# A decoder trunk on one core: the first loads cut and reordered, and another order of recurrent units and gates

## The chip, the cores and the metric

The kernel runs on one core of one Trainium2 chip. The metric is the device time in microseconds (us), the median of several runs. Lower is better.

## What is computed

One inference step of a two-layer decoder trunk on 512 prompt rows and 8 x 8 sample rows of width 1024, all in float32. Cut to what bears on this change, the first layer's first half:

```python
def trunk(x, c, ...):                                  # cut to the start
    sh1, sc1, g1, sh2, sc2, g2 = split(silu(c) @ ada_w[l] + ada_b[l], 6)
    h = rms_norm(x, norm_g[l, 0]) * (1 + sc1) + sh1
    xr, yg = split(h @ w_in, 2)                        # 8 + 8 blocks of 128 columns
    xr, new_buf = causal_dwconv(xr, conv_buf, conv_w, conv_b)        # width 4
    g = sigmoid(einsum('btnc,ncd->btnd', xr by blocks, gate_w) + gate_b)   # r and i
    log_a = 8 * r * log_sigmoid(lam)
    a, u = exp(log_a), sqrt(-expm1(2 * log_a)) * (i * xr)
    o = scan(h -> a * h + u)
    x = x + g1 * ((o * gelu(yg)) @ w_out)
    ...                                                # FFN, K/V, layer 1, final norm
```

## The kernel before

**Layout.** The activations are kept turned, channels on the 128 partitions, in two halves `h` = 0 and 1 of 288 columns (256 prompt rows and 32 sample rows). Prompt row tiles 0, 1 and the samples (tile 4) go to half 0, and tiles 2, 3 to half 1. Turning is done by TensorE (`x_turn`), the sum of squares for the norm by `x_half(h)`: on ScalarE for tiles 0 and 2, on VectorE for tiles 1 and 3.

**Products.** Each float32 weight block is split in two float32r tiles, `hi` (a CAST on ScalarE) and `lo` (raw minus hi, a subtraction on VectorE); `convert` does both for one unit, and the tiles are called `wh`. The activations are split the same way. A product takes three matmuls for each of 8 blocks of 128 rows: hi by xh, hi by xl, lo by xh, each 128x288 (in the profile `mm<-h,wh`). `x01` is a unit pair for columns 0 and 1 of `w_in` (its first unit, blocks 0 to 3, stands at the head of the stream of units; it is tile raw2), `quad` holds rows 0 to 255 of columns 3 to 6 (raw3), whose partial products `quad_parts(h)` puts away in `sl` tiles. The unit loads are 384 or 512 KB each.

**Conditioning.** `ada_first(c, m)` makes scale and shift for two blocks of channels c, c+1 from the raw `ada_w` weights: 64 matmuls of 128x32 by 128 into an `ada` tile, then a transpose. Its weights come by `ada_first_load`, eight loads of 256 KB for a pair: p0 (wh1 to wh4), p1 (wh9 to wh12), p2 (reg6 to reg9), p3. `modulated(h, ...)` then makes h01 (half 0) and h11 (half 1). `wh12b` below is the second load of wh12, the last of p1.

**Recurrent stage.** For each block c of channels: `x` (h by w_in, then the convolution, `evac_xr`), `g` (`gates`: ScalarE CAST ta, VectorE subtraction tb, six 128x300 matmuls `mm<-ta,wh` and `mm<-tb,wh`, then two Tanh, and a Tanh and an Exp that are scaled by the tiles sp2 and nsp4), and `y` (`evac_yg`). sp2 and nsp4 come from `decay_rates`: an Exp of 128x8 on ScalarE, a RECIPROCAL on VectorE, and 24 instructions of 128x8 on GpSimd, the last two of which write sp and nsp.

**Order.** All instructions are recorded in program order, and a list scheduler (`Rec.order`, an `Op` each with `prio`, cost, predecessors) writes each engine's fixed order of issue: at each step it takes the instruction that can start soonest by the planner's costs, weighed with its priority, and looks 24 ahead. The word list `LOADS` sets the order of the first loads on SyncE's queue and of the first conversions (p: ada weights, u: the next unit, x2 and x3: those row tiles). `RNN` sets the order in which x, g and y of each block are recorded. `early(n)` moves an instruction's priority by n places. While TensorE would idle by the plan at the start, fills (128x128 matmuls `mm<-ident`, which nobody reads) are put in. SyncE's queue feeds the 16 DMA engines; the loads are spread over eight DMA rings in turn.

Of the kernel before, what the change touches and what calls it, by code (L numbers as in the profile page):

```python
# [16 lines left out]
ALU = mybir.AluOpType  # L17
AX = mybir.AxisListType

P = 128  # L20
D = 1024
KC = D // P
# [29 lines left out]
SPW = 60  # L52
WIN = 600

LOADS = "p0 u x2 x3 u p1 p201 p223 u u p3"
QUAD = (3, 4, 5, 6)
QK = 2
YT = lambda td, ta, sl: td
RNN = "x0 x1 x2 x3 x4 x5 g0 g1 g2 y2 y0 y1 g3 g4 x6 y3 x7 g5 y5 g6 y6 g7 y4 y7"
ATT = "q0A q2A a0A q1A q0B a2A q1B q3A a0B q2B q4A a1A a1B a4A a3A q3B a2B q5A q4B a3B q6A a5A q5B q7A a6A a4B s0A a5B s1A s2A s3A q6B q7B a7A s0B s1B a6B fA a7B o0A s2B s3B o1A o2A fB"  # L60
LOOK = {"PE": 24, "DVE": 24, "ACT": 24, "POOL": 24, "SP": 24}
NRAW = 4
FILL = 250
DKC = 4
XB = 100
NFILL = 60
AE = 100
A0 = 0.0
# [31 lines left out]
def _is_psum(ap):  # L100
    return str(ap.space).endswith("PSUM")


class Op:
    __slots__ = ("i", "prio", "eng", "emit", "cost", "func", "preds", "succ", "npred", "ready", "allocs", "start", "end", "done", "lat", "tiles", "port", "mode", "idle")


class Ref:
# [39 lines left out]
class Recorder:  # L148
# [57 lines left out]
    def add(self, eng, emit, cost, outs, ins, func=None, lat=0, port=False, mode=0):  # L206
        if self.batch is not None:
            self.mode = mode
            self.batch.append((eng, emit, cost, outs, ins))
            return  # L210
        op = Op()
        op.i = len(self.ops)
        op.prio = op.i + self.bias
        op.eng, op.emit, op.cost, op.func, op.lat = eng, emit, cost, func, lat
        op.port, op.mode, op.idle = port, mode, bool(self.fills) and self.fills[-1][2]
        op.preds, op.succ, op.allocs, op.tiles = set(), [], [], set()
        for ap in self.hold:

            op.preds.update(e[0] for e in self.hist[ap.tensor.name] if e[1])
        for ap, wr in [(x, False) for x in ins] + [(x, True) for x in outs]:  # L220
            if str(ap.space).endswith("DRAM"):
                continue
            for n, p0, p1, lo, hi in self.regions(ap):
                if _is_psum(ap):
                    p0, p1, lo, hi = 0, P, 0, 2048
                op.tiles.add(n)
                h = self.hist.setdefault(n, [])
                if n in self.kind_of and n not in op.allocs:
                    op.allocs.append(n)
                keep = []  # L230
                for e in h:
                    q, ewr, a0, a1, b0, b1 = e
                    if (wr or ewr) and q is not op and a0 < p1 and p0 < a1 and b0 < hi and lo < b1:
                        op.preds.add(q)
                        if wr and p0 <= a0 and a1 <= p1 and lo <= b0 and b1 <= hi:
                            continue
                    keep.append(e)
                keep.append((op, wr, p0, p1, lo, hi))
                self.hist[n] = keep
        self.ops.append(op)  # L240
        return op


    def schedule(self):
# [21 lines left out]
        port, holder, mode = 0.0, "", 0  # L266
# [40 lines left out]
        done = set()  # L307
        fills = deque(self.fills)
        while n_left:
# [67 lines left out]
            _, s, op, sw = best  # L377
# [4 lines left out]
            for n in op.allocs:  # L382
                if n in got:
                    continue
                k = self.kind_of[n]
                c = [u for u in slots[k] if u <= s] or slots[k]
# [3 lines left out]
            cost = op.cost  # L390
            if op.port == 1:
                port, holder = s + cost, e
            elif op.port == 2 and s + 60 < port:
                cost += port - s
            if e == "PE":
                mode = op.mode
# [5 lines left out]
            if op.lat:  # L402

                free[e] = s + op.cost
                if e == "POOL":
                    op.end = s + op.cost + (3000 if op.i < self.strict else 5000)
                else:
                    b = max(s + op.cost + 650, dma_free[0])
                    dma_free[0] = b + op.lat
                    op.end = b + op.lat + (2900 if op.i >= self.strict else 2000)  # L410
            else:
                op.end = free[e] = s + cost
            for n in op.tiles:
# [122 lines left out]
def trunk_kernel(ctx, tc, a):  # L536
    nc = tc.nc
    rec = Recorder(a["shadow"])
    V, S, G, T, Q = (Engine(rec, n, o) for n, o in (("DVE", nc.vector), ("ACT", nc.scalar), ("POOL", nc.gpsimd), ("PE", nc.tensor), ("SP", nc.sync)))
# [19 lines left out]
    raws = Slots(rec, cp, "raw", D, NRAW)  # L559
    whs = Slots(rec, cp, "wh", D, 2 * NHI, F32R)  # L560
# [31 lines left out]
    @contextmanager  # L592
    def early(n):

        rec.bias -= n
        yield
        rec.bias += n
# [14 lines left out]
    ab, ng = a["ada_b"].rearrange("l (r p) -> (l r) p", p=P), a["norm_g"].rearrange("l n (r p) -> (l n r) p", p=P)  # L612
# [20 lines left out]
    ALL = slice(0, P)  # L633

    def x_load(t):
        xt[t] = regs()
        if t < 4:
            Q.dma_start(xt[t].f, a["x_prompt"][0, t * P : (t + 1) * P, :])
        else:
            for q in range(2):  # L640
                Q.dma_start(xt[t].f[64 * q : 64 * q + 64, 0:512], a["x_sample"].rearrange("b t d -> (b t) d")[:, 512 * q : 512 * q + 512])
# [18 lines left out]

    S.activation(tst[1][:, 3:4], ones, AF.Silu)
    x_load(0)
    Q.dma_start(c9.f[0:1, :], a["c_prompt"])
    Q.dma_start(c9.f[1:9, :], a["c_sample"])
# [84 lines left out]
    def ada_w(g):  # L749

        if g in (KVSH, KVSC):
            return a["kv_ada_w"], (g - 6) * D
        return (a["ada_w"][0], g * D) if g < 6 else (a["ada_w"][1], (g - L1) * D)
# [32 lines left out]
    def ada_first_load(c, kind, qs=range(4)):  # L786

        first_w.setdefault(c, [])
        for q in qs:
            b = kind(F32) if kind is whs else kind()  # L790
            first_w[c].append(b)
            for g in (SH1, SC1):
                w, o = ada_w(g)
                src = w[q * 2 * P : (q + 1) * 2 * P, o + c * P : o + (c + 2) * P].rearrange("(k p) n -> p k n", p=P)
                Q.dma_start(b.f[:, 512 * g : 512 * g + 512].rearrange("p (k n) -> p k n", k=2), src)

    def ada_first(c, m):
        o = ps(pada, "ada")
        for q0 in range(0, 4, m):
            with rec.together():  # L800
                for q in range(q0, q0 + m):
                    b = first_w[c][q]
                    for k in range(2):
                        ada_mm(o, 2 * q + k, [b.f[:, n : n + P] for n in (256 * k, 256 * k + P, 512 + 256 * k, 512 + 256 * k + P)], q + k == 0, q + k == 4)
                    b.done()
        t = ada_turn(o, 1, ps(pada, "ada"), td)[:, 0:P].rearrange("p (g c b) -> p g c b", g=2, c=2)
        cs = slice(c, c + 2)
        for k in range(2):
            V.scalar_tensor_tensor(mods[:, SC1, c + k], t[:, SC1, k, 0:9], bias_of(SC1)[:, c + k : c + k + 1], ngT[:, 0, 0, c + k : c + k + 1].to_broadcast([P, 9]), ALU.add, ALU.mult)
        ada_end(SH1, cs, t[:, SH1, :, 0:9])  # L810
# [254 lines left out]
    units = []  # L1065
    nload, nconv = [0], [0]
    nhi = [0]
# [33 lines left out]
    def unit_cols(w, c0, k0=0, kc=KC):  # L1101
        src = w[k0 * P : (k0 + kc) * P, c0 : c0 + P].rearrange("(k p) n -> p k n", p=P)
        u = Unit(kc, [(ALL, slice(0, kc), ALL, src)])
        units.append(u)
        return u

    def unit_pair(w, c0):
        parts = []
        for k0 in (0, 4):
            src = w[k0 * P : (k0 + 4) * P, c0 : c0 + 2 * P].rearrange("(k p) n -> p k n", p=P)  # L1110
            u = Unit(KC, [(ALL, slice(0, 4), slice(0, 2 * P), src)])
            u.n, u.left = 2 * P, 4
            units.append(u)
            parts.append(u)
        return [Half(parts, j) for j in range(2)]
# [167 lines left out]

    seq_ = RNN.split()
    x01 = unit_pair(w_in, 0)
    x2 = unit_cols(w_in, 2 * P)
# [4 lines left out]
    for i, w in enumerate(seq_):  # L1291
        c = int(w[1:])
# [410 lines left out]
    for c in range(KC):  # L1703
# [5 lines left out]
        u = Unit(KC, srcs)  # L1709
# [163 lines left out]
    ready, opened = [[], []], [False, False]  # L1873
# [50 lines left out]
    for m in range(KC):  # L1924
# [6 lines left out]
        u = Unit(KC, srcs)  # L1931
# [5 lines left out]
    for w in ATT.split():  # L1937
        h, n = "AB".index(w[-1]), int(w[1:-1] or 0)
# [86 lines left out]
    def load_one():  # L2025
        load_more(nload[0] - nconv[0] + 1)

    kinds_ = (whs, whs, regs, whs)
    waits = {1: 0, 2: 100, 3: 150, 4: 200}
    n_ = 0  # L2030
    for w in LOADS.split():
        if w[0] == "p":
            ada_first_load(2 * int(w[1]), kinds_[int(w[1])], [int(q) for q in w[2:]] or range(4))
        elif w[0] == "u":
            load_one()
            n_ += 1
            with early(-waits[n_]):
                convert()
        else:
            x_load(int(w[1]))  # L2040
# [4 lines left out]
    for c in range(0, KC, 2):  # L2045
        with early(AE * (c > 0)):
            ada_first(c, AF_[c // 2])
        for h in range(2):
# [4 lines left out]
            if c == 0 and h == 0:  # L2053
                with early(XB):
                    x_half(1)
# [139 lines left out]
```

## Time and profile before

| what | value |
|---|---|
| median of 3 runs | 1243.78 us (1243.7 to 1244.08) |
| the profiled execution | 1243.53 us, its span 1241.8 us |
| granted TensorE clock | 0.999 |
| TensorE (PE) busy | 1230.7 us, 99% of the span |
| VectorE (DVE), ScalarE (ACT), GpSimd (POOL) busy | 894.2, 654.3, 469.5 us |
| HBM read | 160.85 MB, 133 GB/s over the span |

In the rows of the profile a line gives the engine, the operation, and its output and inputs by tile name without buffer numbers. All recorded operations carry the line of one helper (L509), so that tiles, not lines, tell them apart. A group "x10" is ten instructions one behind the other; what stands in brackets is the idle time of the engine ahead of it, and what ended that. PEld is TensorE's weight load, which goes beside the matmuls; SPq is SyncE's queue.

### The profile page before, as it was taken

What the parts mean: (1) busy time and instruction counts of PE and PEld (TensorE: products, weight loads), DVE (VectorE), ACT (ScalarE), POOL (GpSimd) and SP (SyncE); (2) the same over time, 40 slices, a digit from 0 to 9 for tenths busy, and PEclk for the clock granted to TensorE, in tenths of its full rate; (3) what the DMA queues carried; (4) which work ended last, traced back from release to release, by engine and by line L of the source; (5) the groups of instructions that cost most, each with busy time, mean ns of one, the idle gap of its engine ahead of it and who ended that gap; (6) DMA issues with size and microseconds to landing.
All of it is one profiled execution on the core that took longest, in us unless ns stands there. A gap on an engine that the chain in (4) does not pass through costs nothing.

```text
span 1241.8 us, 25378 instructions
## 1 busy us (share of the span) xinstructions
PE 1230.7 (99%) x9592; PEld 1170.2 (94%) x9592; DVE 894.2 (72%) x2137; ACT 654.3 (53%) x1461; POOL 469.5 (38%) x645
## 2 busy tenths in 40 slices
PE   8999999999999999999999999999999999999997
PEld 7888989999999999998999988999999999999997
DVE  5998875896675667477588878568858667757866
ACT  5778954852442454245367679448425435525533
POOL 3264540163441552246135445100436246335500
PEclk9999999999999999999999999999999999999999
DMA  9985554336556555544433221423332323323322
GB/s 314 301 275 168 183 168 139 124 94 195 171 185 207 170 169 183 168 126 157 127 86 71 62 61 53 117 69 110 91 102 73 114 70 103 104 84 86 86 86 77
DMA packets 221164, 165.39 MB, mean 133 GB/s; under 512 B 23817, under 2 KB 205993, under 8 KB 221010
## 3 DMA queue, kind: packets, MB, share of 16 engines
q1 hardware_dynamic: 220434, 163.39, 43.2%
q8 instruction: 75, 1.23, 0.4%
q0 software_dynamic: 608, 0.39, 0.1%
q14 instruction: 47, 0.39, 0.1%
HBM read 160.85 MB, written 4.87 MB: 133 GB/s over the span
## 4 chain that ended last, share of the span: by engine, by line
PE 97%; DMA 1%; DVE 1%; ACT 0%; SPq 0%; issue 0%; DVEq 0%
PE mm L509 91%; PE ada L509 5%; DMA reg<-in_x_prompt_dram 1%; DMA wh<-in_ada_w_dram 0%; DVE h L509 0%; SPq L509 0%; DVE sl L509 0%; DVE tb L509 0%; DVE x L509 0%; DVE wh L509 0%; ACT wh L509 0%; DVE ta L509 0%; DVE mm L509 0%; ACT h L509 0%; ACT x L509 0%
## 5 line engine op out<-in xcount | busy, mean ns | idle before, releaser
L509 PE MATMUL mm<-h,wh 128*128 128x288 f32 x4080 | 583.5, 297 | 0.3
L509 PEld LDWEIGHTS mm<-h,wh 128*128 128x128 f32 x4080 | 552.8, 188 | 12.2 <-issue 6.0
L509 PE MATMUL mm<-sl,wh 128*128 128x288 f32 x3237 | 463.5, 296 | 0.0
L509 PEld LDWEIGHTS mm<-sl,wh 128*128 128x128 f32 x3237 | 439.2, 188 | 5.8 <-issue 5.0
L509 ACT CAST wh<-raw 128x512 fp32r<-128x512 f32 (+3 forms) x394 | 269.8, 706 | 286.1 <-PE mm L509 189.5
L509 DVE TENSOR_TENSOR wh<-raw,wh 128x512 fp32r<-128x512 f32 (+3 forms) x396 | 362.6, 934 | 61.8 <-ACT wh L509 56.6
L509 POOL TENSOR_TENSOR raw<-raw 128x512 f32<-128x512 f32 x78 | 113.9, 1461 | 193.1 <-DVE wh L509 168.8
L509 DVE SCALAR_TENSOR_TENSOR x<-mm,mods,x 128x256 f32<-128x256 f32 x160 | 77.3, 483 | 124.6 <-PE mm L509 123.9
L509 POOL TENSOR_TENSOR x<-x,ta 128x32 f32<-128x32 f32 x120 | 44.1, 367 | 239.8 <-DVE ta L509 237.6
L509 POOL TENSOR_TENSOR raw<-raw,raw 128x512 f32<-128x512 f32 x78 | 118.0, 1513 | 4.5
L509 PE MATMUL mm<-tb,wh 128*128 128x288 f32 (+1 forms) x500 | 92.3, 298 | 0.0
L509 PEld LDWEIGHTS mm<-tb,wh 128*128 128x128 f32 x500 | 74.5, 188 | 2.3 <-DVE wh L509 1.7
L509 POOL TENSOR_TENSOR td<-td,td 128x288 f32<-128x288 f32 x39 | 34.4, 882 | 111.3 <-ACT td L509 98.9
L509 ACT ACTIVATE ta<-x 128x288 f32<-128x288 f32 (+1 forms) x56 | 24.4, 443 | 63.1 <-POOL x L509 41.1
L509 PE MATMUL mm<-ta,wh 128*128 128x288 f32 (+1 forms) x259 | 57.3, 297 | 0.0
L509 DVE TENSOR_TENSOR td<-mm,td 128x288 f32<-128x288 f32 x78 | 34.4, 454 | 26.5 <-PE mm L509 25.9
L509 PE MATMUL ada<-reg,cz 128*32 128x512 f32 (+1 forms) x408 | 47.0, 547 | 0.0
L509 PEld LDWEIGHTS mm<-ta,wh 128*128 128x128 f32 x259 | 42.7, 188 | 1.0 <-ACT ta L509 1.0
L509 DVE TENSOR_TENSOR sl<-td,sl 128x288 fp32r<-128x288 f32 x65 | 39.6, 613 | 3.2 <-ACT sl L509 3.2
L509 ACT CAST sl<-td 128x288 fp32r<-128x288 f32 x65 | 28.0, 433 | 20.1 <-POOL td L509 12.3
L509 ACT ACTIVATE ta<-ta,stat 128x256 f32<-128x256 f32 (+2 forms) x72 | 32.5, 473 | 11.3 <-DVE stat L509 10.4
L509 ACT ACTIVATE td<-td 128x288 f32<-128x288 f32 x39 | 17.3, 443 | 40.1 <-DVE td L509 40.0
(221 smaller groups left out, 1235.9 us busy)
## 6 DMA issues: line engine op xcount, KB each, us to landing
raw<-in_ffn_w_in_dram SPq DMA_DIRECT2D x88, 512.0 KB
reg<-in_ada_w_dram SPq DMA_DIRECT2D x72, 512.0 KB
raw<-in_ffn_w_out_dram SPq DMA_DIRECT2D x32, 384.0 KB
raw<-in_ffn_w_out_dram SPq DMA_DIRECT2D x32, 320.0 KB
reg<-in_kv_ada_w_dram SPq DMA_DIRECT2D x14, 512.0 KB
raw<-in_rnn_w_in_dram SPq DMA_DIRECT2D x13, 512.0 KB
wh<-in_ada_w_dram SPq DMA_DIRECT2D x24, 256.0 KB
raw<-in_rnn_w_out_dram SPq DMA_DIRECT2D x8, 512.0 KB
```

What stands on the lines that cost most here:

```text
L509: self.rec.add(eng, lambda: getattr(obj, name)(*map(real, args), **{k: real(v) for k, v in kw.items()}), cost, outs, ins, func, lat, port, ...
```

## The change

- **Loads.** A first half of raw2 ("a", 256 KB) is loaded and converted by itself (`first_unit`, with priorities W1). raw3, the quad unit, now goes ahead of x2 and x3, and the second half of raw2 ("b") behind x3. In `unit_pair` each unit is loaded by two DMAs of 256 KB, so that raw5, the pair's other unit, has two as well.
- **Norm of half 1.** `x_half(1)` is no longer moved in priority (XB from 100 to 0); its instructions are the same ones. The planner counts the landing of x2 and x3 1.5 us later, and that of each first ada load 0.7 us later (`extra`).
- **Recurrent order.** x5 moves behind the first two gates, and the gates and the y branches stand in another order (`RNN`).

```diff
-LOADS = "p0 u x2 x3 u p1 p201 p223 u u p3"
+LOADS = "p0 a u x2 x3 b p1 p201 p223 u u p3"
+W1 = (0, 100)
+XX, PX = 1500.0, 700.0
-RNN = "x0 x1 x2 x3 x4 x5 g0 g1 g2 y2 y0 y1 g3 g4 x6 y3 x7 g5 y5 g6 y6 g7 y4 y7"
+RNN = "x0 x1 x2 x3 x4 g0 g1 x5 g2 g3 y0 y2 y1 g4 x6 y3 x7 y4 g5 g6 g7 y5 y7 y6"
-XB = 100
+XB = 0
...
-                    op.end = b + op.lat + (2900 if op.i >= self.strict else 2000)
+                    op.end = b + op.lat + (2900 if op.i >= self.strict else 2000) + op.extra
...
+            rec.ops[-1].extra = XX * (t > 1)
...
+                rec.ops[-1].extra = PX * (c == 0)
...
-            u = Unit(KC, [(ALL, slice(0, 4), slice(0, 2 * P), src)])
+            u = Unit(KC, [(ALL, slice(k, k + 2), slice(0, 2 * P), src[:, k : k + 2]) for k in (0, 2)])
...
-    waits = {1: 0, 2: 100, 3: 150, 4: 200}
-    n_ = 0
+    def first_unit(i):
+        u = units[0]
+        if i == 0:
+            u.raw, u.hi, u.lo = raws(), whs(), whs()
+            nload[0] = nconv[0] = nhi[0] = 1
+        t = u.raw.f.rearrange("p (k n) -> p k n", n=u.n)
+        rows, ks, cols, src = u.srcs[i]
+        Q.dma_start(t[rows, ks, cols], src)
+        r = slice(512 * i, 512 * i + 512)
+        with early(-W1[i]):
+            S.copy(u.hi.r[:, r], u.raw.f[:, r])
+            V.tensor_tensor(u.lo.r[:, r], u.raw.f[:, r], u.hi.f[:, r], ALU.subtract)
+        if i == 1:
+            u.raw.done()
+
+    waits = {2: 100, 3: 150, 4: 200}
+    n_ = 1
...
+        elif w[0] in "ab":
+            first_unit("ab".index(w[0]))
```

What the scheduler makes of it, at three places. The orders of all engines differ only in the first part of the program (TensorE's first 1622 of 9023 instructions); from there on they are the same. The number behind a tile's name counts tiles in the program, and differs between the kernels for the same tile; the name and buffer ahead of it can be compared.

TensorE about 25 us into the program, before: the 64 `ada25` matmuls of p1 (wh9 to wh12) and what stands ahead of them; `mm21` is the first product with h11.

```order
L509 MATMUL mm14_420<-h01_330,wh7_389 128x288
L509 MATMUL mm14_420<-h01_330,wh8_408 128x288
L509 MATMUL mm15_455<-h01_330,wh7_389 128x288 x2
L509 MATMUL mm15_455<-h01_330,wh8_408 128x288
L509 MATMUL mm15_455<-h01_330,wh7_389 128x288 x2
L509 MATMUL mm15_455<-h01_330,wh8_408 128x288
L509 MATMUL ada25_470<-wh9_202,cz_78 32x128 x8
L509 MATMUL ada25_470<-wh10_216,cz_78 32x128 x8
L509 MATMUL ada25_470<-wh11_236,cz_78 32x128 x8
L509 MATMUL ada25_470<-wh12_252,cz_78 32x128 x8
L509 MATMUL mm21_524<-h11_487,wh7_389 128x288 x2
L509 MATMUL mm21_524<-h11_487,wh8_408 128x288
```

The same place now:

```order
L512 MATMUL mm20_441<-ident_66,reg5_192 128x128
L512 MATMUL ada25_454<-wh9_209,cz_78 32x128 x8
L512 MATMUL ada25_454<-wh10_222,cz_78 32x128 x8
L512 MATMUL mm29_486<-ident_66,sl7_330 128x8
L512 MATMUL mm35_363<-h01_340,wh5_304 128x288
L512 MATMUL mm35_363<-h01_340,wh6_311 128x288
L512 MATMUL mm33_493<-ident_66,sl2_343 128x80
L512 MATMUL mm35_363<-h01_340,wh5_304 128x288 x2
L512 MATMUL ada25_454<-wh11_240,cz_78 32x128 x8
L512 MATMUL ada25_454<-wh12_256,cz_78 32x128 x8
L512 MATMUL mm21_528<-h11_482,wh7_321 128x288 x2
L512 MATMUL mm21_528<-h11_482,wh8_346 128x288
```

Wherever an order row of `ada25` says x8, the trace shows 16 matmuls. Ahead of `mm21` there stand 36 matmuls of 128x288 before and 29 now: the 24 of the quad unit in both (`mm14` and `mm15` are two of its four columns), and 12 or 5 of the x01 unit (now `mm35`). Two small transposes, `mm29` and `mm33`, which came behind `mm21` and its row before, now come ahead of it.

TensorE at the first gate, before: `mm45` and `mm46` take ta25 and tb25, the gate's two operands, and `mm44` is the last x unit ahead of it (18 matmuls, x5).

```order
L509 MATMUL mm44_1104<-h01_330,wh26_1029 128x288
L509 MATMUL mm45_1141<-ta25_977,wh27_1003 128x300
L509 MATMUL mm45_1141<-ta25_977,wh28_1090 128x300
L509 MATMUL mm45_1141<-tb25_1113,wh27_1003 128x300
L509 MATMUL mm46_1149<-ta25_977,wh27_1003 128x300
L509 MATMUL mm46_1149<-ta25_977,wh28_1090 128x300
L509 MATMUL mm46_1149<-tb25_1113,wh27_1003 128x300
```

And now:

```order
L512 MATMUL mm43_1061<-h11_482,wh14_694 128x288
L512 MATMUL mm44_1118<-ta25_970,wh25_981 128x300
L512 MATMUL mm44_1118<-ta25_970,wh26_1031 128x300
L512 MATMUL mm45_1124<-ta25_970,wh25_981 128x300
L512 MATMUL mm45_1124<-ta25_970,wh26_1031 128x300
L512 MATMUL mm44_1118<-tb25_1115,wh25_981 128x300
L512 MATMUL mm45_1124<-tb25_1115,wh25_981 128x300
```

The 18 matmuls of x5's half 0 have moved behind the gates of blocks 0 and 1, and the first use of tb25 stands behind four matmuls with ta25 instead of two.

ScalarE at the Exp of `decay_rates` (tile sl16, 128x8), before: two casts and an activation stand between it and the copies of `mm43`.

```order
L509 CAST ta29_1026<-sl19_942 128x300
L509 ACTIVATE sl21_1034<-td9_968,vecT_73 128x300
L509 ACT_TABLE_LOAD
L509 ACTIVATE sl16_120<-sl16_120 128x8
L509 CAST ta31_1051<-sl20_956 128x300
L509 ACTIVATE sl23_1094<-td11_1010,vecT_73 128x300
L509 CAST wh29_1108<-raw12_922 128x1024
L509 COPY td12_1031<-mm43_1054 128x256
L509 COPY td12_1031<-mm43_1054 128x4x8
L509 ACTIVATE sl24_1132<-td12_1031,vecT_73 128x300
```

And now:

```order
L512 COPY td12_1033<-mm43_1061 128x256
L512 COPY td12_1033<-mm43_1061 128x4x8
L512 ACTIVATE sl24_1140<-td12_1033,vecT_73 128x300
L512 CAST ta35_1152<-sl22_1028 128x300
L512 ACT_TABLE_LOAD
L512 ACTIVATE sl16_120<-sl16_120 128x8
L512 ACTIVATE ta26_1176<-mm44_1118,hgb_81 128x300
L512 ACTIVATE tb26_1184<-mm45_1124,hgb_81 128x300
L512 ACTIVATE ta28_1191<-mm46_1131,hgb_81 128x300
L512 ACTIVATE tb28_1198<-mm47_1136,hgb_81 128x300
```

The Exp has moved from ahead of the copies of `mm43` to behind them, just ahead of the first gate's Tanh. The row that first needs its result comes 13 rows behind the Exp in both (rows 94 before and 103 now, `ACTIVATE sl<-ta,sp`), the eight activations of the first two blocks' gates then stand in one piece, and 17 rows behind that first one stands the `CAST ta37` of a later gate (block 4, half 1).

More of the change, by code (lines that the diff above doesn't have):

```diff
@@ L104 @@
 class Op:
-    __slots__ = ("i", "prio", "eng", "emit", "cost", "func", "preds", "succ", "npred", "ready", "allocs", "start", "end", "done", "lat", "tiles", "port", "mode", "idle")
+    __slots__ = ("i", "prio", "eng", "emit", "cost", "func", "preds", "succ", "npred", "ready", "allocs", "start", "end", "done", "lat", "tiles", "port", "mode", "idle", "extra")
 class Ref:
@@ L214, in add @@
         op.eng, op.emit, op.cost, op.func, op.lat = eng, emit, cost, func, lat
+        op.extra = 0.0
         op.port, op.mode, op.idle = port, mode, bool(self.fills) and self.fills[-1][2]
```

## The prediction

> **What bounds the kernel now.** I read the page first, then TensorE's waits, then its timeline up to where they end. The page's span and its row of busy times:
>
> ```profile
> span 1241.8 us, 25378 instructions
> PE 1230.7 (99%) x9592; PEld 1170.2 (94%) x9592; DVE 894.2 (72%) x2137; ACT 654.3 (53%) x1461; POOL 469.5 (38%) x645
> ```
>
> TensorE (PE) is the bound. The two longest of the five waits that the trace finds on it:
>
> ```profile
> PE mm L509 <- DMA reg<-in_x_prompt_dram: 1.9, 1, 1.9
> PE mm L509 <- POOL few L590: 1.4, 1, 1.4
> ```
>
> The second belongs to the fills that open the program. The first, 1.9, lies where the loads' order touches; here is PE's timeline there (start, busy time, what):
>
> ```profile
> 15.82 1.26 PE L509 MATMUL mm<-ident 128*128 128x128 f32 x10
> 18.94 1.06 PE L509 MATMUL mm<-ident,reg 128*128 128x128 f32 x8 [1.87 <-DMA reg<-in_x_prompt_dram]
> 20.11 0.27 PE L509 MATMUL mm<-ident 128*128 128x128 f32 x1
> 22.50 0.38 PE L509 MATMUL mm<-ident 128*128 128x128 f32 x2
> 23.85 0.38 PE L509 MATMUL mm<-ident 128*128 128x128 f32 x2
> 24.21 1.59 PE L509 MATMUL mm<-h,wh 128*128 128x288 f32 x10
> 27.37 1.96 PE L509 MATMUL ada<-wh,cz 128*32 128x128 f32 x64
> 29.26 0.81 PE L509 MATMUL mm<-h,wh 128*128 128x288 f32 x4
> 32.75 0.63 PE L509 MATMUL mm<-ident,sl 8*128 8x8 f32 x3
> 33.31 0.93 PE L509 MATMUL mm<-h,wh 128*128 128x288 f32 x5
> 34.08 0.23 PE L509 MATMUL mm<-ident,sl 80*128 80x80 f32 x1
> 34.11 0.38 PE L509 MATMUL mm<-h,wh 128*128 128x288 f32 x1
> ```
>
> The rows `mm<-ident` without a second tile are fills, which nobody reads. The last stand at 23.85. After them PE is never free, by the busy times of two stretches (columns: stretch, its length, then PE busy):
>
> ```profile
> 24.00:40.00 16.00, 16.00 (x213) 14.30 (x211) 12.91 (x50) 10.62 (x25) 2.09 (x3) 1.00 1.08 332
> 40.00:58.00 18.00, 18.00 (x182) 17.22 (x181) 16.98 (x57) 12.74 (x33) 5.34 (x17) 1.00 1.00 324
> ```
>
> So, of what the change touches, only the waits and fills up to 24.2 us can be won; from there every new wait of PE adds its whole length. Of useful work PE gets the same amount (fills apart). What decides is how much of that work is left when PE stops waiting for good.
>
> **Term 1, the first stage.** The quad unit goes ahead of x2 and x3, so PE has 24 matmuls to do where it waited 1.87 us. That wait goes. What is late next? The 64 `ada25` matmuls need wh12b, the last of p1's eight loads, and the change only permutes what lies ahead of it: the same bytes. Two casts that wait for their loads show the stream's pace (ScalarE's timeline; the DMA share below is of one window, from 16.0 to 28.5 us):
>
> ```profile
> 16.01 1.05 ACT L509 CAST wh<-raw 128x1024 fp32r<-128x1024 f32 x1 [0.41 <-DMA raw<-in_rnn_w_in_dram]
> 36.12 1.05 ACT L509 CAST wh<-raw 128x1024 fp32r<-128x1024 f32 x1 [1.56 <-DMA raw<-in_rnn_w_in_dram]
> DMA packets 3957, 4.31 MB, mean 345 GB/s; under 512 B 423, under 2 KB 3530, under 8 KB 3955
> ```
>
> From raw2 (16.0) to raw4 (36.1) the queue holds 24 pieces of 256 KB (x2, x3 and quad two each, p1 and p2 eight each, raw4 two): 20.11 / 24 = 0.84 us each. wh12b is the 14th: 16.0 + 11.7 = 27.7. Counted back from raw4, ten pieces at 345 GB/s (0.76 us each): 28.5. PE's last 16 of `ada25` (a quarter of 29.26 - 27.37 = 1.89, so 0.47) can't start before; with a switch of 0.2, `mm21` starts between 28.4 and 29.2. Before it started at 29.26 and PE came to wh12b about when it landed. I take 29.2, as a load counted near its end is the safer count.
>
> By then the new order has done seven matmuls of 128x288 less (29 for 36). One costs 0.136 us, by the 42 from 60.12 to 65.83 (quoted below), so 0.95 us is owed. In exchange `mm29` and `mm33` are done: the three small transposes hold PE from 32.75 to 33.31, of which one and its switch is 0.2 to 0.37; `mm33` 0.12 (five matmuls from 33.31 end at 33.99, the next starts at 34.11). I take 0.45 for both. **Net +0.5 us**, in the form of PE waiting 1.1 to 1.3 us ahead of the second half of `ada25`, where it had none. Should wh12b not be what is late, PE's own work sets `mm21`: before, 18.94 to 29.26 holds 10.3 us, less 0.9 of fills, less 0.5 as above, is 8.9; begun at 18.2 (the h01 that both use) with 0.8 us for the quad's lo part, which the cast of a later load delays: 27.9, that is 1.35 early and 0.5 owed: -0.85. So the term lies between -0.85 and +0.6.
>
> The two more loads on SyncE's queue (raw2 and raw5 are cut) cost an issue each. Rows of the loads behind them (ns, least, median and most):
>
> ```profile
> L509 SPq DMA_DIRECT2D reg<-in_ada_w_dram x8: 367/368/1143, 22.5 to 28.5; - x8
> ```
>
> 0.37 us of queue, hidden as the queue runs ahead of the landings by some pieces; 0 here. The Trainium skill, DMA: Bandwidth & Descriptors, section Bandwidth, says the opposite of halving: batch DMAs to 1 MiB or more; by its fixed cost of about 2.0 us a DMA (Anatomy of one DMA) the one cut load ahead of wh12b would make this sum 2 us worse. The rows side with the queue: p1 and p2 are all in pieces of 256 KB, and 345 GB/s flow.
>
> The norm: the description speaks of three VectorE instructions; in the diff `x_half` keeps all it had and only its place changes. No gain is counted there.
>
> **Term 2, the first gates.** They now come ahead of x5. Timelines of PE, then VectorE:
>
> ```profile
> 58.26 1.92 PE L509 MATMUL ada<-reg,cz 128*32 128x512 f32 x16
> 60.12 5.88 PE L509 MATMUL mm<-h,wh 128*128 128x288 f32 x42
> 65.83 0.44 PE L509 MATMUL mm<-ta,wh 128*128 128x300 f32 x2
> 66.11 0.30 PE L509 MATMUL mm<-tb,wh 128*128 128x300 f32 x1
> 63.80 0.46 DVE L509 TENSOR_TENSOR tb<-sl,ta 128x300 fp32r<-128x300 f32 x1
> ```
>
> Eighteen of the 42 move behind the gates: they begin at 65.83 - 18 x 0.136 = 63.4, four ta matmuls (0.14 each) bring PE to tb25 at 63.95, and tb25 is done at 64.26: 0.3 us of waiting if both shift alike, none if only PE is 0.5 late, 0.5 if VectorE has more ahead of it. **I take +0.2.**
>
> **Term 3, the decay rates.** The Exp moves behind the casts and the copies of `mm43`, and a chain on GpSimd hangs on it. ScalarE, then GpSimd (its first, a slow, a quick and the last step), and VectorE's first wait behind them:
>
> ```profile
> 58.85 1.28 ACT L509 ACT_TABLE_LOAD   x1
> 60.15 0.21 ACT L509 ACTIVATE sl<-sl 128x8 f32<-128x8 f32 x1
> 65.00 0.64 ACT L509 ACTIVATE sl<-td,vecT 128x300 f32<-128x300 f32 x1
> 70.08 0.50 ACT L509 ACTIVATE ta<-mm,hgb 128x300 f32<-128x300 f32 x1
> 70.48 0.50 ACT L509 ACTIVATE tb<-mm,hgb 128x300 f32<-128x300 f32 x1
> 72.61 0.64 ACT L509 ACTIVATE sl<-ta,sp 128x300 f32<-128x300 f32 x1 [1.30 <-POOL sp L509]
> 61.12 1.09 POOL L509 TENSOR_TENSOR sl<-sl 128x8 f32<-128x8 f32 x3 [0.32 <-DVE sl L509]
> 62.30 1.23 POOL L509 TENSOR_SCALAR sl<-sl 128x8 f32<-128x8 f32 x1
> 66.87 0.23 POOL L509 TENSOR_SCALAR sl<-sl 128x8 f32<-128x8 f32 x1
> 72.66 0.23 POOL L509 TENSOR_SCALAR nsp<-sl 128x8 f32<-128x8 f32 x1
> 73.81 0.47 DVE L509 SCALAR_TENSOR_TENSOR tb<-sl,sl 128x300 f32<-128x300 f32 x1 [1.62 <-ACT sl L509]
> ```
>
> From the Exp to nsp: 72.89 - 60.15 = 12.7 us, with steps of 1.0 to 1.2 us among others of 0.2 to 0.5; with every step near 0.3, 24 steps take about 7.5, and 8.5 with what precedes them. On ScalarE an instruction takes 0.1 less than its busy time when others queue behind it (70.08 to 70.48 for 0.50). Now the Exp comes after the activation at 65.00 (0.54), a cast as wide as a Tanh (0.4) and a table load (1.28): at 67.2. nsp is ready between 75.7 and 79.9.
>
> When is it wanted? Gates at 64.1 (terms 1 and 2 in), 12 matmuls of 0.14, 36 of 0.136, an ada row (1.86, from 58.26 to 60.12), 12 and 18 more: 76.7; there a weight tile comes free, whose CAST (1.05) stands ahead of the first `sl<-ta,sp`: 77.7. So ScalarE is late by 0 to 2.2 us. Behind it 13 activations at 0.54 and four Tanh at 0.4 bring it to the `CAST ta37` at about 86.3, done at 86.7; PE takes ta37 after 24 matmuls, 12 of gates, 24 and 18, at 87.3. The cover is 0.4 to 0.6; what exceeds it PE waits: 0 to 1.8. With nsp midway, at 77.8, it would wait for nothing, at three quarters, 78.9, for 0.8. **I take +0.3**, between these two.
>
> From GpSimd's row at 62.30 (1.23, beside a VectorE subtraction) against 66.87 (0.23) a mechanism speaks: GpSimd stands still through such subtractions. The Trainium skill, SBUF — State Buffer, section SBUF: two separate sides, has a rule for it: the pair of ports is an exclusive lock for a whole instruction, and VectorE with two SBUF inputs takes it. By that rule, with VectorE as dense as before, the long end would hold; this is rival B.
>
> **Sum.** 0.5 + 0.2 + 0.3 = +1.0: 1244.5 against the profiled execution's own 1243.53 (span 1241.8 and 1.7 around it). The median of before is 0.25 higher, so I say **1244.8**.
>
> **The rivals.**
> - A, the first stage does win: wh12b lands by 27.2 and terms 2 and 3 are near 0. For it, the lost wait of 1.87 and 0.9 us of fills; against it, the pace above. Term 1 -0.85: 1242.9. Chance 0.17.
> - B, slower: ScalarE waits for nsp at its first `sl<-ta,sp`, and PE for ta37 at `mm62`. It decides from nsp at 79.9 on: PE waits 79.9 - 77.7 - 0.4 = 1.8, with 0.5 and 0.2 it is 2.5; with a chain one us longer, 3.5: 1246.3 to 1247.3. For it, VectorE's density; against it, VectorE fell idle at 72.2 before (73.81 less 1.62), while ScalarE waited for sp, and the chain's second part would then be quick. Chance 0.17.
> - C, the cut load ahead of wh12b delays the stream by its issue, 0.37: 1245.2. Chance 0.03. It would bear out the Trainium skill's rule on batching (DMA: Bandwidth & Descriptors, Bandwidth) in sign, not in size.
> - D, all terms larger on the good side than I see. All fills and the wait ahead of `mm21` (1.87 + 1.26 + 0.9, 4.0) would have to go, though wh12b at 27.7 allows 1.4 at most. Chance 0.04.
> - The change doesn't do what it says (the norm): 0 us, within the forecast.
>
> **How the numbers follow.** The forecast has 0.59, A 0.17, B 0.17, C 0.03, D 0.04. A measurement of this kernel tells about 0.2%, 2.5 us, from no change. Faster than 1241.3 is D alone, 0.04; slower than 1246.3 is B, 0.17; the rest, 0.79, is the same. The range takes in A (less 0.3 for a shorter term 1) and most of B: 1242.6 to 1247.2.
>
> **What would show it.** Right: PE's wait for x2 is gone, a wait of about 1.2 us for an ada load stands in its place near 27 us, and `mm21` starts near 29.2; a wait of 0.2 us for tb near 64; the Exp near 67 and the last GpSimd step between 76 and 80. Wrong: `mm21` at 28 or earlier (A); a wait of PE for ta near 87 of over 1 us (B); any new wait past 100 us, where both orders are the same.

## The result, and the profile after

The changed kernel takes 1245.99 us (median of 13 runs, 1245.29 to 1250.8) against 1243.7 us of before beside it (13 runs, 1242.81 to 1245.85): a ratio of 1.002, 95% interval 1.0012 to 1.0028. That is +2.3 us, slower in sign, just inside the 0.2% that I had called "the same", and more than twice the +1.0 that was forecast. The profiled execution took 1245.99 us, its span is 2.4 us longer than before's. The page's span, and the first rows of what TensorE (PE) waits for:

```profile
span 1244.2 us, 25388 instructions
```

```profile
PE mm L512 <- POOL few L593: 1.4, 1, 1.4
PE mm L512 <- ACT ta L512: 1.1, 2, 1.0
PE mm L512 <- DMA sl<-in_ada_b_dram: 0.9, 1, 0.9
PE mm L512 <- ACT h L512: 0.6, 1, 0.6
PE ada L512 <- ACT td L512: 0.3, 1, 0.3
```

The wait for x2 (1.9) is gone, as the diff means it to. New are 1.0 us in one piece for a `ta`, and a short one of an `ada` transpose for `td`. The first stage, PE's timeline:

```profile
18.88 0.93 PE L512 MATMUL mm<-h,wh 128*128 128x288 f32 x5 [0.61 <-ACT h L512]
20.12 2.92 PE L512 MATMUL mm<-h,wh 128*128 128x288 f32 x20
...
25.25 1.08 PE L512 MATMUL ada<-wh,cz 128*32 128x128 f32 x32
...
27.27 1.46 PE L512 MATMUL ada<-wh,cz 128*32 128x128 f32 x32
28.65 0.80 PE L512 MATMUL mm<-h,wh 128*128 128x288 f32 x4
...
37.19 0.33 PE L512 MATMUL ada<-ident,td 128*128 128x128 f32 x1 [0.31 <-ACT td L512]
```

The second half of `ada25` takes 1.38 us to the next row, where 32 matmuls make 0.94 at the pace of before (1.89 for 64): 0.4 us go to wh12. `mm21` starts at 28.65. The other wait is at 37.19, behind this stretch of ScalarE:

```profile
35.92 1.05 ACT L512 CAST wh<-raw 128x1024 fp32r<-128x1024 f32 x1 [1.97 <-DMA raw<-in_rnn_w_in_dram]
36.88 0.26 ACT L512 COPY td<-ada 128x128 f32<-128x128 f32 x1
```

The copy that PE waits for stands behind a cast that waits for raw4. The gates (PE):

```profile
63.80 0.71 PE L512 MATMUL mm<-ta,wh 128*128 128x300 f32 x4
64.35 0.44 PE L512 MATMUL mm<-tb,wh 128*128 128x300 f32 x2
...
81.26 5.91 PE L512 MATMUL mm<-h,wh 128*128 128x288 f32 x42
88.15 0.54 PE L512 MATMUL mm<-ta,wh 128*128 128x300 f32 x2 [0.98 <-ACT ta L512]
88.71 0.40 PE L512 MATMUL mm<-tb,wh 128*128 128x300 f32 x1
```

No wait for tb at 64. At 88.15 PE takes ta37: the 42 matmuls ahead of it end their turn at 81.26 + 42 x 0.136 = 86.97, so 1.2 us are lost, and 0.3 more for tb37 (0.56 between the last two rows, 0.28 elsewhere). ScalarE there, then GpSimd and VectorE:

```profile
67.43 0.21 ACT L512 ACTIVATE sl<-sl 128x8 f32<-128x8 f32 x1
...
76.47 1.05 ACT L512 CAST wh<-raw 128x1024 fp32r<-128x1024 f32 x1 [0.88 <-PE mm L512]
79.19 0.64 ACT L512 ACTIVATE sl<-ta,sp 128x300 f32<-128x300 f32 x1 [1.67 <-POOL sp L512]
...
87.66 0.44 ACT L512 CAST ta<-sl 128x300 fp32r<-128x300 f32 x1
```

```profile
72.63 0.23 POOL L512 TENSOR_SCALAR sl<-sl 128x8 f32<-128x8 f32 x1
72.94 0.20 POOL L512 TENSOR_TENSOR sl<-sl 128x8 f32<-128x8 f32 x1
...
73.55 1.23 POOL L512 TENSOR_TENSOR sl<-sl 128x8 f32<-128x8 f32 x1
...
77.59 1.25 POOL L512 TENSOR_TENSOR sl<-sl 128x8 f32<-128x8 f32 x1
78.93 0.23 POOL L512 TENSOR_SCALAR sp<-sl 128x8 f32<-128x8 f32 x1
```

```profile
73.49 1.23 DVE L512 TENSOR_TENSOR wh<-raw,wh 128x1024 fp32r<-128x1024 f32 x1 [0.42 <-ACT wh L512]
...
77.55 1.23 DVE L512 TENSOR_TENSOR wh<-raw,wh 128x1024 fp32r<-128x1024 f32 x1 [0.31 <-ACT wh L512]
```

sp is written at 79.2 and ScalarE wanted it at 77.5: 1.67 us late, then 16 more instructions in order, then the `CAST ta37`. Two of GpSimd's steps lie beside a weight subtraction of VectorE and last as long as it (1.23 and 1.25, against 0.20 and 0.23 elsewhere). The Trainium skill, SBUF — State Buffer, section SBUF: two separate sides, says that the shared pair of ports is an exclusive lock for a whole instruction when VectorE has two SBUF inputs and GpSimd reads SBUF; these rows agree.

**Where the 2.4 us of span went.** I counted, from the starts of all matmuls in each trace, when PE had done the same useful work (fills left out), against before's first profile. The columns are four such amounts of work, which before has done at 40, 94, 219 and 1226 us (us later than before):

| kernel | 40 | 94 | 219 | 1226 |
|---|---|---|---|---|
| before, second profile | 0.1 | 0.0 | 0.1 | 0.3 |
| changed | 0.3 | 2.0 | 1.8 | 2.6 |
| changed, second profile | 3.8 | 5.3 | 5.1 | 5.9 |
| changed, short series (e4_skip) | 0.3 | 0.2 | 0.4 | 0.8 |
| changed, series on VectorE (e9_dve) | 0.3 | 1.1 | 0.8 | 1.6 |
| changed, sp's readers later (e5_cost400) | -0.5 | -0.5 | 0.3 | 1.1 |
| before, long chain (e6_long) | 2.0 | 5.2 | 5.2 | 5.4 |

Of the changed kernel's 2.6, the first stage has 0.3, the stretch from 40 to 94 us has 1.7 (1.5 of it at ta37), and 0.6 come slowly behind 900 us, where the orders of both kernels are the same and the trace finds no wait. That the second profile of the changed kernel and e6_long are 3.8 and 2.0 us late by 40 us already has another cause, told with those runs.

### The profile page after: what moved, and what is told of

It is laid out like the page before. It is cut to its first block, busy times and chain, and to the rows that moved or that the text cites. A ratio compares the mean times of both kernels' runs of the same rounds, so it can differ in the third digit from the quotient of the medians.

```text
span 1244.2 us, 25388 instructions
## 1 busy us (share of the span) xinstructions
PE 1232.6 (99%) x9596; PEld 1171.0 (94%) x9596; DVE 894.5 (72%) x2138; ACT 651.8 (52%) x1461; POOL 465.8 (37%) x645
## 3 DMA queue, kind: packets, MB, share of 16 engines
q8 instruction: 75, 1.23, 0.4%
## 4 chain that ended last, share of the span: by engine, by line
PE 91%; DVE 1%; ACT 0%; issue 0%; DVEq 0%
PE mm L512 87%; PE ada L512 4%; DVE wh L512 0%; DVE h L512 0%; DVE sl L512 0%; DVE tb L512 0%; DVE x L512 0%; DVE ta L512 0%; DVE mm L512 0%; ACT h L512 0%; ACT ta L512 0%; DVE td L512 0%; ACT sl L512 0%; DVEq L2213 0%; DVE few L512 0%
## 5 line engine op out<-in xcount | busy, mean ns | idle before, releaser
L512 DVE TENSOR_TENSOR wh<-raw,wh 128x512 fp32r<-128x512 f32 (+4 forms) x397 | 363.9, 934 | 64.8 <-ACT wh L512 59.8
L512 ACT ACTIVATE td<-td 128x288 f32<-128x288 f32 x39 | 17.3, 444 | 40.3 <-DVE td L512 40.3
```

What stands on the lines that cost most here:

```text
L512: self.rec.add(eng, lambda: getattr(obj, name)(*map(real, args), **{k: real(v) for k, v in kw.items()}), cost, outs, ins, func, lat, port, ...
```

## The experiments

The theory: **PE loses 1.5 us because ScalarE, in order, waits for sp ahead of the `CAST ta37`, and sp is late since the Exp moved and the chain takes 11 us.** The rivals: the order of gates costs it by itself (eight activations in one piece); the first stage costs it. Ratios are to runs of before on the same chip.

**e4_skip: the chain cut, all orders kept.**

```diff
         for n in range(15, 0, -2):
...
+                if 5 <= n <= 13:
+                    rec.ops[-1].emit = lambda: None
```

The two lines stand behind each of the loop's two instructions: both are planned as before, but not issued for n = 13 to 5.

> The changed kernel with every engine's order kept, but GpSimd leaves out five of the eight steps of the series in decay_rates (ten instructions of 128x8; sp and nsp are then less exact). Theory (PE waits 1.5 us for ta37 because sp and nsp come late): sp is ready near 75, ScalarE's wait of 1.67 ahead of its first sl<-ta,sp and PE's wait of 0.98 for ta37 are gone, time 1.2 to 1.5 us below the changed kernel, so +0.8 to +1.1 on the kernel before. Rival (ScalarE is late through its eight activations in one piece, whatever GpSimd does): PE still waits over 0.7 us for ta37, time as the changed kernel, +2.3 on before.

1244.74 us, ratio 1.0008 (0.9999 to 1.0016), +1.2 on before and so a little above the +0.8 to +1.1 that was expected. ScalarE's first reader of sp, then PE at ta37:

```profile
77.28 0.63 ACT L512 ACTIVATE sl<-ta,sp 128x300 f32<-128x300 f32 x1
```

```profile
81.12 5.74 PE L512 MATMUL mm<-h,wh 128*128 128x288 f32 x42
86.70 0.44 PE L512 MATMUL mm<-ta,wh 128*128 128x300 f32 x2
```

No wait on either, and in the table the loss between 40 and 94 us is gone (0.3, then 0.2). The eight activations are still in one piece, so that rival falls.

**e6_long: the reverse, before with a longer chain, all orders kept.**

```diff
         G.tensor_tensor(w2, w_, w_, ALU.mult)
+        again = rec.ops[-1].emit
+        rec.ops[-1].emit = lambda: [again() for _ in range(9)]
```

> The kernel before, every order kept, with one GpSimd step of decay_rates (w2 = w * w) done nine times, eight more instructions of 128x8 that change no value. Theory (in-order ScalarE passes a late sp on to PE in either order of gates): sp comes 3 to 5 us later, near 76 to 78, ScalarE's wait of 1.30 grows to 4 to 6, and PE waits 1 to 4 us for a ta or a weight cast by 90 us: +1 to +4 on before. Rival (the old order of gates has the cover): PE waits under 0.3 us more, 0 to +0.3.

1246.72 us, ratio 1.0025 (1.0016 to 1.0035); the profiled execution, 1248.94, was one of the slowest. GpSimd's eleven steps, ScalarE's wait, and PE's:

```profile
62.88 6.44 POOL L509 TENSOR_TENSOR sl<-sl 128x8 f32<-128x8 f32 x11 [0.32 <-DVE sl L509]
```

```profile
77.12 0.64 ACT L509 ACTIVATE sl<-ta,sp 128x300 f32<-128x300 f32 x1 [4.05 <-POOL sp L509]
```

```profile
83.25 0.54 PE L509 MATMUL mm<-h,wh 128*128 128x288 f32 x2 [0.57 <-ACT wh L509]
84.69 4.67 PE L509 MATMUL mm<-h,wh 128*128 128x288 f32 x22 [0.89 <-DVE wh L509]
89.15 0.53 PE L509 MATMUL mm<-ta,wh 128*128 128x300 f32 x2
```

Here a weight cast behind the waiting activation is what PE misses, and PE falls back by 3.2 us (2.0 to 5.2 in the table). The two waits are less than half of it, 0.57 and 0.89. The 22 matmuls from 84.69 to 89.15 take 4.46 us, where 22 at 0.136 make 3.0: 13 of them come 0.24 us apart, and the granted clock from 86.00 to 89.15 is 0.50. e3_early50 (82.3 to 85.7) and e8_cost400_px1000 have such a stretch near their waits too; e1_rnn, e2_loads and the changed kernel have waits of PE here and no such stretch, so what brings it on is not shown. The old order of gates too hands a late sp on; before had sp 1.3 us late and this cost nothing, 4.05 cost three.

**e9_dve: the series computed in full, on VectorE.** In GpSimd's places nine VectorE instructions stand, eight of which add a constant and multiply in one.

```diff
+        def horner(m, by):
+            if m is None:
+                V.obj.tensor_tensor(real(s_), real(s_), real(by), ALU.mult)
+            else:
+                V.obj.scalar_tensor_tensor(real(s_), real(s_), m, real(by), ALU.add, ALU.mult)
...
             G.tensor_tensor(s_, s_, w2, ALU.mult)
+            rec.ops[-1].emit = lambda m=last[0]: horner(m, w2)
             G.tensor_scalar(s_, s_, 1.0 / n, None, ALU.add)
+            rec.ops[-1].emit = lambda: None
+            last[0] = 1.0 / n
```

> The changed kernel, every other instruction in its place, with the series of decay_rates computed in full by nine VectorE instructions (add a constant and multiply in one) where GpSimd had seventeen. Theory (the chain's length is the loss): sp comes near 76 to 77, ScalarE's wait for it is under 0.5, PE's wait for ta37 under 0.3, time 0.9 to 1.4 us below the changed kernel, +0.8 to +1.3 on before. Rival (nine more instructions on a busy VectorE make its weight subtractions late): sp early, but PE waits over 0.5 us for a wh or tb, time as the changed kernel.

1245.81 us, ratio 1.0013 (1.0005 to 1.0022): some of the loss comes back, less than expected. By the times alone this isn't certain, as the changed kernel had 1.0018 (1.0009 to 1.0027) beside it; the trace shows it. GpSimd's last step, and ScalarE and PE behind it:

```profile
77.69 1.06 POOL L512 TENSOR_SCALAR nsp<-sl 128x8 f32<-128x8 f32 x1
```

```profile
77.64 0.64 ACT L512 ACTIVATE sl<-ta,sp 128x300 f32<-128x300 f32 x1 [0.24 <-POOL sp L512]
```

```profile
87.22 0.54 PE L512 MATMUL mm<-ta,wh 128*128 128x300 f32 x2 [0.34 <-ACT ta L512]
```

sp is 0.24 late, nsp another 0.5, since its one instruction fell beside a subtraction (77.43, 1.23). PE loses 0.8 instead of 1.7. With less lateness of sp and nsp PE loses less, as the theory has it.

**e5_cost400: sp's readers behind ta37.** The planner counts 0.4 us for each GpSimd instruction of the chain; by its own costs it counts 0.10 (tensor_scalar) to 0.17 (tensor_tensor).

```diff
+        for o in rec.ops[n0:]:
+            if o.eng == "POOL":
+                o.cost = 400.0
         tw.done()
```

> The changed kernel, with the planner counting 0.4 us for each GpSimd instruction of decay_rates (the trace shows 0.2 to 1.25), so that it puts all activations that read sp behind the CAST ta37 that PE waits for; the orders ahead of the first gates stay. Theory (PE waits only since ta37 stands in ScalarE's queue behind the wait for sp): PE's wait for ta37 is gone though sp still comes near 79, and the time is 0.8 to 1.5 us below the changed kernel, +0.8 to +1.5 on before. Rival (GpSimd's lateness reaches PE by another way, the scan and the y branches): PE waits elsewhere by 92 us, +2 or more.

1245.59 us, ratio 1.0018 (1.0009 to 1.0027); its profiled run was among its faster ones (1244.49). There, on ScalarE and then PE:

```profile
82.16 0.47 ACT L512 CAST ta<-sl 128x300 fp32r<-128x300 f32 x1
82.49 3.30 ACT L512 ACTIVATE sl<-ta,sp 128x300 f32<-128x300 f32 x6
```

```profile
85.98 0.44 PE L512 MATMUL mm<-ta,wh 128*128 128x300 f32 x2
```

PE doesn't wait for ta37 though sp is written only at 78.4: the way by which the lateness reaches PE is ScalarE's order, as expected. The time missed: the median is +2.0 on before, not +0.8 to +1.5, and can't be told from the changed kernel's. That is the rival's size, but not its mechanism, as the trace has no wait of PE for these readers by 92 us. Part of it is seen in the table: 0.8 us are given back between 94 and 219 us, where the new plan has other orders.

**e3_early50 and e1_rnn: the Exp early, with the new order of gates.** The first is the changed kernel with `decay_rates` recorded 50 places earlier, the second is before with the new `RNN` line alone.

```diff
-            decay_rates()
+            with early(50):
+                lambdas()
+                decay_rates()
```

> The changed kernel with decay_rates recorded 50 places earlier, so that the Exp stands ahead of the copies of mm43 again. Theory (late nsp): the Exp comes near 60 to 62, sp near 73 to 75, no wait of PE for ta over 0.3 us, +0.4 to +0.9 on the kernel before (what is left of the first stage). Rival (order of gates costs it): +2.3.

> The kernel before with the new order of recurrent units and gates alone; the scheduler puts the Exp ahead of the copies of mm43 here. Theory (the loss needs the late Exp, not the gate order): sp near 73, PE waits under 0.5 us for ta, -0.2 to +0.6 on the kernel before. Rival (the gate order alone): +1.3 to +2.

Both missed: 1249.14 us (1.0043, 1.003 to 1.0055) and 1246.18 us (1.0022, 1.0013 to 1.0032), each above its rival's figure too. ScalarE and PE of e1_rnn, then of e3_early50:

```profile
73.77 0.64 ACT L509 ACTIVATE sl<-ta,sp 128x300 f32<-128x300 f32 x1 [6.63 <-POOL sp L509]
```

```profile
81.75 0.93 PE L509 MATMUL mm<-h,wh 128*128 128x288 f32 x5 [1.32 <-ACT wh L509]
```

```profile
72.74 0.64 ACT L512 ACTIVATE sl<-ta,sp 128x300 f32<-128x300 f32 x1 [5.88 <-POOL sp L512]
```

```profile
80.72 3.55 PE L512 MATMUL mm<-h,wh 128*128 128x288 f32 x17 [1.71 <-ACT wh L512]
```

sp did come near 73, as expected. But the planner, which counts the chain short, moved its readers up as well, to right behind the first gates' Tanh, and ScalarE stood 6 us with weight casts behind it. "The Exp is early" was the wrong thing to ask for; what counts is sp's time against the place of its first reader. The new `RNN` line alone thus costs as much as the whole change, by the same kind of wait at another place.

**e2_loads: the first stage alone, with the old `RNN` line.**

> The first stage of the change alone, with the old order of recurrent units and gates. Theory: PE behind by 0.35 us after 40 us as in the changed kernel, no wait for ta over 0.3 us, +0.2 to +0.7 on the kernel before. Rival (the first stage makes most of the loss): +1.5 to +2.3.

1249.49 us, ratio 1.0045 (1.0032 to 1.0057), above both expectations. It does not isolate what it should: the planner made another order of the gates and y branches too, and the larger part of its loss is there. PE's two largest waits:

```profile
37.97 0.33 PE L512 MATMUL ada<-ident,td 128*128 128x128 f32 x1 [1.47 <-ACT td L512]
...
88.08 0.53 PE L512 MATMUL mm<-h,wh 128*128 128x288 f32 x2 [2.21 <-ACT td L512]
```

By its place the first is the raw4 wait again; in this run the cast ahead of the copy started at 36.71 (the profile names a load of ada weights as what ended its wait). PE's order up to there is that of the changed kernel, and yet PE is 1.1 us behind before at 40 us.

**e8_cost400_px1000: PE kept at work while wh11 and wh12 land.** e5's edit, and p1's loads counted 1 us later, which puts the 24 products of h11 ahead of the second half of `ada25`.

```diff
-                rec.ops[-1].extra = PX * (c == 0)
+                rec.ops[-1].extra = PX * (c == 0) + 1000.0 * (c == 2)
```

> The changed kernel with the planner's 0.4 us for each GpSimd instruction of decay_rates, and with p1's loads counted 1.0 us later, which puts the 24 products of h11 ahead of the second half of ada25 and the Exp 38 places further ahead on ScalarE. Theory: no wait for sp that reaches PE, and PE works while wh11 and wh12 land: -0.5 to +0.5 on before. Rival 1 (the next load, raw4, holds PE at the following ada turn all the same): +0.3 to +0.8. Rival 2 (the planner's new order opens other waits on ScalarE): +1.5 or more.

1255.89 us, ratio 1.0097 (1.0083 to 1.0111). The largest piece is one wait of 5.6 us of PE for a `td` at 127 us, where in the new order ScalarE has stood 3.98 us ahead of a cast for VectorE; some 3 us are lost by 94 us already, with a wait of 1.46 for a `wh` at 87 us (rival 2). Its first stage is what I wanted to see, on PE:

```profile
26.42 3.97 PE L512 MATMUL mm<-h,wh 128*128 128x288 f32 x27
30.32 1.08 PE L512 MATMUL ada<-wh,cz 128*32 128x128 f32 x32
...
37.32 0.33 PE L512 MATMUL ada<-ident,td 128*128 128x128 f32 x1 [1.25 <-ACT td L512]
```

No wait for wh12 is left, and PE is some 0.8 us ahead of before by 31 us; at 37.32 it has to give all of it back, as the cast of raw4 (from 36.05) stands ahead of the copy. That is rival 1.

**e7_bcost400: before with the same prices.**

> The kernel before with the planner's 0.4 us for each GpSimd instruction of decay_rates. Theory: before's wait of ScalarE for sp cost PE nothing, so nothing is to be won: -0.3 to +0.5 on before, with the wait of 1.30 under 0.5. Rival (that wait did reach PE in a way that the waits don't show): -1.0 or lower.

1247.16 us, ratio 1.0029 (1.0018 to 1.0041), outside both expectations' ranges. Up to 98 us PE keeps before's pace to 0.2 us; the loss of 3 us comes behind, in the new order (the largest piece 1.53 us for a tb at 146 us). It tells nothing of the chain, only that a correct price alone doesn't make a better plan.

**Both kernels once more.**

> The changed kernel once more, for a second profile. Theory: PE waits 0.8 to 1.3 us for ta37 near 88 again, with sp near 79; the place where PE stands at 40 us moves by up to 0.7 us from profile to profile, as the first loads land. Rival (the wait near 88 was that run's alone): under 0.3.

> The kernel before once more, for a second profile: the ada turn behind the first cast of raw4 at 37.4 in the first profile. Theory (the first stage's difference is no larger than the spread of the loads): it comes between 37.2 and 38.2, and PE waits for no ta or sp near 88. Rival (the first stage costs a fixed +0.3): within 0.1 of 37.4.

The changed kernel: 1246.67 us (1.0018, 1.0009 to 1.0027); before: 1243.6 us (0.9997, 0.9988 to 1.0006). ScalarE and PE of the changed kernel's second profile, then PE of before's:

```profile
82.46 0.64 ACT L512 ACTIVATE sl<-ta,sp 128x300 f32<-128x300 f32 x1 [1.67 <-POOL sp L512]
```

```profile
91.42 0.55 PE L512 MATMUL mm<-ta,wh 128*128 128x300 f32 x2 [0.96 <-ACT ta L512]
```

```profile
37.43 0.33 PE L509 MATMUL ada<-ident,td 128*128 128x128 f32 x1 [0.43 <-ACT td L509]
```

The second profile of the changed kernel is 3.5 us later than the first by 40 us, where up to 0.7 was expected, and yet has the same waits (1.67 and 0.96). Its delay isn't one of the loads: the eight transposes `mm<-ident,reg` from 7.55 us took 1.97 us there and 1.09 in the first profile, the eleven from 11.64 took 2.61 and 1.42, and the trace's records of the granted clock begin with the full clock at 17.3 us, in the first profile at 6.0. e6_long began in the same way (14.2 us, in before 5.9). Before's second profile was 0.5 us ahead of the first at 34 us and level with it at 37.4: there too the cast of raw4 sets the place. That place fits the theory and the rival alike and decides nothing between them.

Before's second profile shows one thing more, on ScalarE:

```profile
73.23 0.64 ACT L509 ACTIVATE sl<-ta,sp 128x300 f32<-128x300 f32 x1 [1.91 <-POOL sp L509]
```

Here sp is 1.91 us late for its first reader, more than the 1.67 of the changed kernel, and PE loses nothing (0.0 at 94 us in the table). So the two kernels do not differ in how late sp is, but in the cover: in the old order ScalarE can stand for 1.9 us before PE misses anything, in the new one for about 0.5. The loss needs both, the late sp and the new order; without the lateness the new order costs nothing there (e4_skip).

## Why the prediction was right in its range and wrong in the sizes of its terms

- **Term 1 (+0.5).** Measured +0.3, in the trace of the changed kernel, e4_skip and e9_dve alike. But the step "what is late next is wh12b" holds only in part: it cost 0.4 us, `mm21` came at 28.65 and not 29.2, and the place was set later, by raw4, through the cast that stands ahead of the copy of `ada27` on ScalarE. e8_cost400_px1000 shows it: without the wait for wh12 the same place comes no earlier. I had followed one load and not the next one that a queue waits for. With the same order of TensorE up to this place, e5_cost400 was 0.5 us ahead of the kernel before at 40 us and e2_loads 1.1 behind it, as the cast of raw4 started at 35.09 and 36.71; so +0.3 lies within the spread, and a fixed cost of the first stage is not shown.
- **Term 2 (+0.2).** Measured 0: tb25 came in time.
- **Term 3 (+0.3).** This is the step that failed. The place, the chain, the wait of ScalarE, and PE waiting for ta37 all came as rival B put them; nsp was ready at 79.5, inside "between 75.7 and 79.9", and wanted at 77.5 (77.7). I had discounted the long end by "VectorE fell idle at 72.2 before ... the chain's second part would then be quick". In the new order two weight subtractions, at 73.49 and 77.55, lie in just that part and hold the chain for 2 us. The chain as a whole did not grow, 12.0 us from the Exp to nsp where before had 12.7; it was the discount on that length that was wrong, and with nsp at 79.5 the prediction's own sum gives a wait of 1.4. Measured, the wait of ScalarE was 1.67, of which 0.5 was covered as I had it, 1.2 reached PE, and 0.3 came on top by tb37, which hangs on the cast of ta37 and which I had left out. 1.5 for 0.3.
- **Sum.** 0.3 + 0 + 1.5 = 1.8, and the trace has 2.0 at 94 us and 1.8 to 2.0 from 219 to 900 us; the rest up to 2.3 to 2.6 is the slow drift at the end, which is not explained.
- **Range.** That the time fell into the range is in part luck. What came was rival B, which had a chance of 0.17, and its sign, a wait of PE for ta near 87 of over 1 us, was met at the edge: 0.98 in the row at 88.15, 1.2 by the count. Terms 1 and 2 came out 0.4 us smaller than forecast and term 3 1.2 larger, and a drift that nobody had forecast filled up the rest.
- **The cut loads (rival C).** In the changed kernel 4.30 MB flow at 344 GB/s between 16.0 and 28.5 us, before 4.31 MB at 345: no cost of the halving shows, and nothing of the 2 us that the Trainium skill's fixed cost a DMA (DMA: Bandwidth & Descriptors, Anatomy of one DMA) would have made of it. That section has the cost for DMAs that GpSimd issues, and these loads come from SyncE's queue.

What the runs did not point to is a version that beats the kernel before: its late sp costs it nothing, and every new plan lost elsewhere.

## What to carry to other kernels

A dependent chain of tiny instructions on an engine that nobody watches can set the pace of the bound engine, through an in-order engine that has the chain's reader ahead of what the bound engine needs: compare the chain's end with the place of its first reader, and count what stands behind it. An equal wait can cost nothing in one order (1.91 us in before) and 1.5 us in another (1.67 here). Cost such a chain by the order of after, with the neighbour's long instructions that will lie beside it, not by the idle time that the neighbour had before. When a wait on a load is filled with work, look for the next load behind which another queue waits.

## What I had not expected

- GpSimd's 128x8 steps stand still for the whole of a VectorE subtraction (1.23 and 1.25 us for 0.20 to 0.23), and twice in one chain this makes the difference between covered and not.
- Moving a producer earlier made the kernel slower (e3_early50, +5.6 us on before where the changed kernel has +2.3), since the planner's too short price of the chain moved the readers further than the producer.
- The place of PE at 37 to 40 us moves from run to run with the first loads, between 0.5 us ahead of before and 1.1 behind it in the same order, more than the whole first stage was worth.
- A wait of PE can cost more than its length: in e6_long, waits of 0.57 and 0.89 us were followed by 3.15 us at a granted clock of 0.50, which cost another 1.5.
- Behind 900 us the changed kernel loses 0.6 us against before with the same orders and without waits; e4_skip (0.6) and e9_dve (0.5) show it too, before's second profile 0.1. It is spread over some 2500 matmuls, none of which follows the one ahead of it by more than 0.02 us later than in before. What causes it stays open.
